# Row maxima on one core: six late rows moved from VectorE to TensorE and GpSimd, and the loads cut to 22

## The chip, the cores and the metric

The kernel runs on one core of a Trainium2 chip. The metric is the device time of one execution in microseconds (us); lower is better. Beside it stands the span: the time from the first to the last instruction that the profile of that execution shows. The time is longer than the span; the difference is called "outside the span". Faster or slower needs 2%.

## The reference

```python
# x: float32 [32, 512, 1024]
def reference(x):
    return np.max(x, axis=-1).astype(np.float32)      # [32, 512]
```

There are 16,384 rows of 1,024 values, 67.1 MB. They lie over 128 partitions, 128 rows on each. Below, "a row" means one row on each partition: 512 KB and one column of the result.

## The kernel before

All of x passes once through a ring of 45 rows in SBUF. Each load brings n rows, and VectorE reduces a whole load in one instruction. The loads get smaller so that little is left to do when the last one lands; the last row comes in two halves.

```python
BLOCKS = [
    [14, 13, 12, 11, 9, 8, 8, 7, 6, 5, 5, 4, 4, 3, 3],
    [2, 2, 2, 1, 1, 1, 1, 1, 1, 1, 1, 1],
]
RING = 45
# ...
        for n in loads:
            if at + n > RING:
                at = 0
            xc = ring[:, at:at + n, :]
            nc.sync.dma_start(out=xc, in_=xb[:, b:b + n, :])
            reduce = nc.vector.reduce_max(out=res[:, first + b:first + b + n], in_=xc, axis=X)
            at += n
            b += n
# ... the last row in two halves, then two small stores of the result
```

Of the kernel before, what the change touches and what calls it, by code (L numbers as in the profile page):

```python
# [1 line left out]

# [4 lines left out]


F32 = mybir.dt.float32



BLOCKS = [
    [14, 13, 12, 11, 9, 8, 8, 7, 6, 5, 5, 4, 4, 3, 3],
    [2, 2, 2, 1, 1, 1, 1, 1, 1, 1, 1, 1],
]
RING = 45
SYNC = mybir.DependencyInfo(mybir.DependencyClass.Sync, mybir.DependencyReason.DATA)


@with_exitstack
def kernel(
    ctx: ExitStack,
    tc: tile.TileContext,
    x: bass.AP,
    out: bass.AP,
):
    nc = tc.nc
    P = 128
    X = mybir.AxisListType.X  # L30

    xf = x.flatten_outer_dims()
    N, D = xf.shape
    H = D // 2
    I = N // P
    of = out.flatten_outer_dims()

    once = ctx.enter_context(tc.tile_pool(name="once", bufs=1))
    ring = once.tile([P, RING, D], F32)
    res = once.tile([P, I], F32)  # L40

    PAD = 16
    tail = once.tile([P, PAD + H], F32)

    at = first = 0
    views = []
    for loads in BLOCKS:
        S = sum(loads) + (loads is BLOCKS[-1])
        xb = xf[first * P:(first + S) * P, :].rearrange("(p i) d -> p i d", p=P)
        dst = bass.AP(tensor=of.tensor, offset=of.offset + first * P, ap=[[S, P], [1, S]])  # L50
        views.append((dst, res[:, first:first + S]))
        b = 0
        for n in loads:
            if at + n > RING:
                at = 0
            xc = ring[:, at:at + n, :]
            nc.sync.dma_start(out=xc, in_=xb[:, b:b + n, :])  # L57
            reduce = nc.vector.reduce_max(out=res[:, first + b:first + b + n], in_=xc, axis=X)  # L58
            at += n
            b += n  # L60
        first += S
    assert first == I

    if at + 1 > RING:
        at = 0
    half = ring[:, at, :H]
    nc.sync.dma_start(out=half, in_=xb[:, b, :H])
    nc.sync.dma_start(out=tail[:, PAD:], in_=xb[:, b, H:])
    nc.vector.reduce_max(out=tail[:, PAD - 1:PAD], in_=half, axis=X)  # L69
    nc.vector.reduce_max(out=res[:, I - 1:], in_=tail[:, PAD - 1:], axis=X)  # L70


    store = nc.scalar.dma_start(out=views[0][0], in_=views[0][1])
    tc.add_manual_dep(store.ins, reduce.ins.name, SYNC, reason="behind the loads")
    nc.scalar.dma_start(out=views[1][0], in_=views[1][1])


# [1 line left out]
_INS = ['x']  # L79
_OUTS = [((32, 512), 'float32')]  # L80


# [23 lines left out]
```

## Time and profile before

| | before |
|---|---|
| time, median | 165.02 us (6 runs, 164.87 to 165.15) |
| span | 163.4 us |
| VectorE busy | 139.0 us in 29 instructions |
| input stream, first to last byte | 1.72 to 159.29 us |
| last reduction ends | 161.07 us |

How to read it: neither share of busy time decides. VectorE (DVE in the profile) is busy for 85% of the span, but nearly all its idle time (20.3 of 22.1 us) lies at the start, before the first load has landed. The input stream occupies the 16 DMA engines almost from start to end (96.6% of the span, queue q1 of the page). What counts is which of the two finishes last: VectorE, at 161.07 us, less than 2 us behind the last byte. After it come the store of the result and the end of the program, 2.3 us. The lines are shown in the prediction.

### The profile page before, as it was taken

To read this page: it belongs to the slowest core of one execution; us is meant where nothing else is said; L and a number is where in the kernel's file an instruction comes from. 1 tells how busy PE (TensorE), PEld (TensorE's weight loads), DVE (VectorE), ACT (ScalarE), POOL (GpSimd) and SP (SyncE) were. 2 spreads that over 40 slices of the span, in tenths; PEclk is the share of its full clock that TensorE was granted. 3 is DMA by queue.
4 is the path that set the end of the run, shared out by engine and by line. 5 is a ranking of instruction groups with operands and counts; after the bars stand their busy time and mean duration, and the time that the engine had idled before them with its cause. 6 is when DMAs were issued, how large, how long until landed. Compare 5 with 4: busy or idle time off the path is not lost.

```text
span 163.4 us, 117 instructions
## 1 busy us (share of the span) xinstructions
DVE 139.0 (85%) x29; POOL 0.2 (0%) x4
## 2 busy tenths in 40 slices
DVE  0000099989998999999999999999999999999994
POOL 0000000000000000000000000000000000000000
DMA  6999999999989989999989999999999999999990
GB/s 225 449 449 449 433 417 417 417 401 529 433 385 430 452 386 432 433 433 441 457 385 481 401 442 422 409 438 421 446 409 425 437 410 422 427 407 409 409 355 16
DMA packets 4464, 67.18 MB, mean 411 GB/s; under 512 B 752, under 2 KB 752, under 8 KB 2160
## 3 DMA queue, kind: packets, MB, share of 16 engines
q1 hardware_dynamic: 4176, 67.11, 96.6%
q10 hardware_dynamic: 288, 0.07, 0.2%
HBM read 67.11 MB, written 0.07 MB: 411 GB/s over the span
## 4 chain that ended last, share of the span: by engine, by line
DVE 49%; DMA 48%; SPq 1%; issue 0%
DMA ring<-in_x_dram 48%; DVE res L58 48%; SPq L57 1%; DVE res L70 0%; DVE tail L69 0%
## 5 line engine op out<-in xcount | busy, mean ns | idle before, releaser
L58 DVE TENSOR_REDUCE res<-ring 128x1 f32<-128x1024 f32 (+12 forms) x27 | 137.7, 5165 | 22.1 <-DMA ring<-in_x_dram 22.1
L70 DVE TENSOR_REDUCE res<-tail 128x1 f32<-128x513 f32 x1 | 0.7, 686 | 0.0
L69 DVE TENSOR_REDUCE tail<-ring 128x1 f32<-128x512 f32 x1 | 0.7, 682 | 0.0
L90 POOL MEMSET const-bfloat16-1.0<- 128x1 bf16 x1 | 0.1, 102 | 0.0
L90 POOL MEMSET const-uint8-127<- 128x1 uint8 x1 | 0.1, 102 | 0.0
L90 POOL MEMSET const-float32-0.0<- 128x1 f32 x1 | 0.1, 99 | 0.2 <-issue 0.2
L90 POOL MEMSET const-float32-1.0<- 128x1 f32 x1 | 0.1, 99 | 0.0
## 6 DMA issues: line engine op xcount, KB each, us to landing
ring<-in_x_dram SPq DMA_DIRECT2D x2, 4096.0 KB, 25.6
ring<-in_x_dram SPq DMA_DIRECT2D x1, 7168.0 KB, 19.6
ring<-in_x_dram SPq DMA_DIRECT2D x1, 6656.0 KB, 34.9
ring<-in_x_dram SPq DMA_DIRECT2D x1, 6144.0 KB, 48.9
ring<-in_x_dram SPq DMA_DIRECT2D x1, 5632.0 KB, 28.5
ring<-in_x_dram SPq DMA_DIRECT2D x2, 2560.0 KB, 38.4
ring<-in_x_dram SPq DMA_DIRECT2D x1, 4608.0 KB, 24.7
ring<-in_x_dram SPq DMA_DIRECT2D x9, 512.0 KB, 13.8
```

Of the source, the lines that this page charges most:

```text
L57: nc.sync.dma_start(out=xc, in_=xb[:, b:b + n, :])
L58: reduce = nc.vector.reduce_max(out=res[:, first + b:first + b + n], in_=xc, axis=X)
L69: nc.vector.reduce_max(out=tail[:, PAD - 1:PAD], in_=half, axis=X)
L70: nc.vector.reduce_max(out=res[:, I - 1:], in_=tail[:, PAD - 1:], axis=X)
L90: nc = _bacc.Bacc("TRN2", target_bir_lowering=False, num_devices=1)
```

## The change

The intent is to take work from VectorE late in the kernel, where it is behind, by the three engines that stand idle (the page of the kernel before has no busy time on TensorE and ScalarE and 0.2 us on GpSimd). Each of six rows is turned on TensorE (eight transposes of 128x128, so that the values of one row lie across partitions), copied from PSUM to SBUF by ScalarE, reduced over partitions by GpSimd, and its 8 x 128 partial maxima are turned back on TensorE (eight one-column transposes). VectorE then reduces 8 values instead of 1,024. With less work, VectorE was to stand fewer and larger loads, 22 in place of 29.

```diff
 BLOCKS = [
-    [14, 13, 12, 11, 9, 8, 8, 7, 6, 5, 5, 4, 4, 3, 3],
-    [2, 2, 2, 1, 1, 1, 1, 1, 1, 1, 1, 1],
+    [(15, 0, -1), (15, 0, -1), (15, 0, -1), (15, 0, -1), (12, 0, -1), (7, 0, -1), (11, 0, -1), (10, 2, 8), (7, 0, -1), (5, 2, 13)],
+    [(4, 1, 15), (2, 0, -1), (2, 1, 18), (1, 0, -1), (1, 0, -1), (1, 0, -1), (1, 0, -1), (1, 0, -1), (1, 0, -1), (1, 0, -1)],
 ]
-RING = 45
+RING = 46
 ...
+    def by_gpsimd(rows, cols, m):
+        back = psmall.tile([P, m, C], F32)
+        for k in range(m):
+            ps = psum.tile([P, D], F32)
+            for c in range(C):
+                in_turn("PE", nc.tensor.transpose(out=ps[:, c * P:(c + 1) * P], in_=rows[:, k, c * P:(c + 1) * P], identity=ident))
+            sb = turn.tile([P, D], F32)
+            nc.scalar.copy(out=sb, in_=ps)
+            top = allr.tile([P, D], F32)
+            nc.gpsimd.partition_all_reduce(top, sb, P, bass_isa.ReduceOp.max)
+            run(backs)                 # turns back of the row before
+            backs.append(turn_back)    # turn_back: eight transposes of top[0:1, ...] into back[:, k, c]
+        return lambda: in_turn("DVE", nc.vector.reduce_max(out=cols, in_=back, axis=X))
 ...
             if m:
                 due.setdefault(w, []).append(by_gpsimd(...))
+            else:
+                run(backs)
+            if j == 0:
+                nc.gpsimd.tensor_copy(out=ident[:, 0:1], in_=xc[:, 0, 0:1])
+                make_identity(nc, ident)
```

A triple (n, m, w) means: load n rows, send the last m of them through the detour, and let VectorE take in their results after its reduction of load w. `in_turn` fixes the order of the instructions on TensorE and on VectorE.

More of the change, by code (lines that the diff above doesn't have):

```diff
@@ L6 @@
 from concourse._compat import with_exitstack
+from concourse import bass_isa
+from concourse.masks import make_identity
 F32 = mybir.dt.float32
 BLOCKS = [
-    [14, 13, 12, 11, 9, 8, 8, 7, 6, 5, 5, 4, 4, 3, 3],
-    [2, 2, 2, 1, 1, 1, 1, 1, 1, 1, 1, 1],
-]
-RING = 45
+    [(15, 0, -1), (15, 0, -1), (15, 0, -1), (15, 0, -1), (12, 0, -1), (7, 0, -1), (11, 0, -1), (10, 2, 8), (7, 0, -1), (5, 2, 13)],
+    [(4, 1, 15), (2, 0, -1), (2, 1, 18), (1, 0, -1), (1, 0, -1), (1, 0, -1), (1, 0, -1), (1, 0, -1), (1, 0, -1), (1, 0, -1)],
+]
+RING = 46
+NOSYNC = mybir.DependencyInfo(mybir.DependencyClass.NoSync, mybir.DependencyReason.DATA)
 SYNC = mybir.DependencyInfo(mybir.DependencyClass.Sync, mybir.DependencyReason.DATA)
@@ L34 @@
     H = D // 2
+    C = D // P
     I = N // P
@@ L38, with in_turn, turn_back, run @@
     once = ctx.enter_context(tc.tile_pool(name="once", bufs=1))
+    turn = ctx.enter_context(tc.tile_pool(name="turn", bufs=2))
+    allr = ctx.enter_context(tc.tile_pool(name="allr", bufs=2))
+    psum = ctx.enter_context(tc.tile_pool(name="psum", bufs=3, space=bass.MemoryType.PSUM))
+    psmall = ctx.enter_context(tc.tile_pool(name="psmall", bufs=2, space=bass.MemoryType.PSUM))
     ring = once.tile([P, RING, D], F32)
     res = once.tile([P, I], F32)
+    ident = once.tile([P, P], F32)
     PAD = 16
     tail = once.tile([P, PAD + H], F32)
-    at = first = 0
+    backs = []
+    due = {}
+    before = {}
+    def in_turn(engine, inst):
+        if engine in before:
+            tc.add_manual_dep(inst.ins, before[engine].ins.name, NOSYNC, reason="in turn")
+        before[engine] = inst
+        return inst
+    def by_gpsimd(rows, cols, m):
[3 more added lines that the diff above has]
+            for c in range(C):
+                in_turn("PE", nc.tensor.transpose(
+                    out=ps[:, c * P:(c + 1) * P],
+                    in_=rows[:, k, c * P:(c + 1) * P],
+                    identity=ident,
+                ))
+            sb = turn.tile([P, D], F32)
[3 more added lines that the diff above has]
+            run(backs)
+            def turn_back(top=top, k=k):
+                for c in range(C):
+                    in_turn("PE", nc.tensor.transpose(
+                        out=back[:, k, c:c + 1],
+                        in_=top[0:1, c * P:(c + 1) * P],
+                        identity=ident[0:1, 0:1],
+                    ))
+            backs.append(turn_back)
+        return lambda: in_turn("DVE", nc.vector.reduce_max(out=cols, in_=back, axis=X))
+    def run(calls):
+        while calls:
+            calls.pop(0)()
+    at = first = j = 0
     views = []
     for loads in BLOCKS:
-        S = sum(loads) + (loads is BLOCKS[-1])
+        S = sum(n for n, m, w in loads) + (loads is BLOCKS[-1])
         xb = xf[first * P:(first + S) * P, :].rearrange("(p i) d -> p i d", p=P)
@@ L52 @@
         b = 0
-        for n in loads:
+        for n, m, w in loads:
             if at + n > RING:
@@ L57 @@
             nc.sync.dma_start(out=xc, in_=xb[:, b:b + n, :])
-            reduce = nc.vector.reduce_max(out=res[:, first + b:first + b + n], in_=xc, axis=X)
+            cols = res[:, first + b:first + b + n]
+            if m:
+                due.setdefault(w, []).append(by_gpsimd(xc[:, n - m:, :], cols[:, n - m:], m))
+            else:
[3 more added lines that the diff above has]
+                make_identity(nc, ident)
+            if n > m:
+                reduce = in_turn("DVE", nc.vector.reduce_max(
+                    out=cols[:, :n - m], in_=xc[:, :n - m, :], axis=X))
+            run(due.get(j, []))
             at += n
             b += n
+            j += 1
         first += S
     assert first == I
-    if at + 1 > RING:
-        at = 0
     half = ring[:, at, :H]
@@ L68 @@
     nc.sync.dma_start(out=tail[:, PAD:], in_=xb[:, b, H:])
-    nc.vector.reduce_max(out=tail[:, PAD - 1:PAD], in_=half, axis=X)
-    nc.vector.reduce_max(out=res[:, I - 1:], in_=tail[:, PAD - 1:], axis=X)
+    in_turn("DVE", nc.vector.reduce_max(out=tail[:, PAD - 1:PAD], in_=half, axis=X))
+    in_turn("DVE", nc.vector.reduce_max(out=res[:, I - 1:], in_=tail[:, PAD - 1:], axis=X))
     store = nc.scalar.dma_start(out=views[0][0], in_=views[0][1])
```

## The prediction

> **What bounds the kernel now.** I read the busy shares by slice first, then the chain that ended last in order of time, then the groups of instructions kept apart by shape, then the busy time by stage, and last the single DMA packets.
>
> The page's slices (columns: forty equal slices of 4.1 us, busy share in tenths):
>
> ```profile
> DVE  0000099989998999999999999999999999999994
> DMA  6999999999989989999989999999999999999990
> ...
> q1 hardware_dynamic: 4176, 67.11, 96.6%
> ```
>
> Two rows are full at once. The DMA engines run from the first slice to the last, VectorE from the sixth. Neither has a hole that the other could be moved into. The chain that ended last, in order of time (start, length, what):
>
> ```profile
> 1.63 48.93 DMA ring<-in_x_dram
> 50.56 0.02 issue
> 50.58 12.96 DVE res L58
> ...
> 63.94 30.30 DMA ring<-in_x_dram
> 94.24 0.02 issue
> 94.27 65.48 DVE res L58 x21
> 159.75 0.60 DVE tail L69
> 160.35 0.02 issue
> 160.38 0.69 DVE res L70
> ```
>
> Up to 94.24 us the path goes through the DMA, after it through VectorE alone. So VectorE sets the end: 21 reductions back to back without a wait, done at 161.07 us. But the DMA is close behind. The single packets show the last data byte of the input at 159.29 us, after 1.72 us for the first, and the 16 engines idle for under 0.8 us in between. The last half row was issued at 150.77 us and took 9.0 us to land, so it landed at 159.77 us. Had VectorE been infinitely ahead, its last half-row reduction of 0.69 us would have ended near 160.5 us. **Taking work from VectorE can win about 0.6 us** before the stream takes over. In the groups below (columns: busy us, mean ns, idle time before and what ended it) most of its idle time, 20.3 of 22.1 us, is the wait for the first load.
>
> ```profile
> L58 DVE TENSOR_REDUCE res<-ring 128x14 f32<-128x14336 f32 x1 | 15.1, 15086 | 20.3 <-DMA ring<-in_x_dram 20.3
> L58 DVE TENSOR_REDUCE res<-ring 128x1 f32<-128x1024 f32 x9 | 10.2, 1215 | 0.0
> L70 DVE TENSOR_REDUCE res<-tail 128x1 f32<-128x513 f32 x1 | 0.7, 686 | 0.0
> ```
>
> Rates from here: (15,086 - 1,215)/13 = 1.067 us a row, plus about 0.15 us an instruction, of which some 0.09 overlap with the next when nothing is waited for (1-row reductions start every 1.125 us).
>
> ```profile
> 100.00:150.00 50.00, 50.00 (x13) 0.00 (x0) 1.00 1.00 421
> ```
>
> In this stage (columns: stretch, length, DVE busy, POOL busy, PE clock, DMA share, GB/s) both are at 100%.
>
> [...]a 57,344-byte packet takes 2.115 us, 27.1 GB/s an engine, 434 for 16. A 4,096-byte packet takes 0.161 us (407 GB/s), so a packet costs some 0.010 us beside its bytes.
> [...]
> [...]
> [...]
>
> **The change, part by part.**
> *DMA stream.* The bytes stay. 29 loads become 22, at 8 packets per engine each: 56 packets fewer per engine, by 0.010 us: **-0.5 us**. A row per partition is 8 packets of 4,096 bytes, 1.204 us; a load adds 0.08. The first load took 1.3 us longer than that (18.2 us for 14 rows); I keep that. The new stream ends at about 158.8 us and the last half row lands at about 159.2 (0.4 to 0.5 us after its last byte). I walked the ring of 46 rows through: the fourth load waits for the first reduction, at 37.7 us, but the second and third keep the queue full until 57.4; no later load is short either, nor does the limit of 8 loads in flight that the issues wait for bite. The stream stays unbroken.
>
> *VectorE's start.* The first load has 15 rows, not 14: it lands at 21.6, 1.2 us later. The first four loads are all of 15. The DMA needs 18.1 us for each, VectorE 16.15, so VectorE waits 2.0 us before each of the second, third and fourth (landings 39.7, 57.8, 76.0). In the kernel before, shrinking loads left it only 0.65, 0.51, 0.38 and 0.21. VectorE is then idle for 21.6 + 5.9 + some 0.4 later = 27.9 us against 22.1: **+5.8 us**.
>
> *VectorE's work.* Six rows leave: 6 x 1.067 = 6.4 us. The 27 big reductions become 20. Their fixed part is 2.2 us before (139.0 less 127 rows at 1.067 and the two halves, 1.3 net), and 4 x 0.15 + 16 x 0.06 = 1.6 after: -0.6. Four little reductions of the turned-back maxima come in, 16 or 8 values each, estimated at 0.16 us: +0.65. Together **-6.4 us** (139.0 to 132.6).
>
> *Sum.* From 92.1 us (end of the fourth reduction) VectorE has 62 rows left: 66.1, plus 18 instructions at 0.06, plus 0.65, plus 0.4 of waits: end at 160.4, against 161.07. The two sums agree: -6.4 + 5.8. So **-0.65 us if the six maxima arrive in time**. Time: 164.99 - 0.65 = 164.3 us.
>
> *The detour.* Each late row costs 8 turns on TensorE (p), a ScalarE copy of 1,024 columns (c[...]), the all-reduce (T) and 8 one-column turns back (b). VectorE's order is fixed, so it stands still if a result is late. The order of instructions shows the tight place. The two rows of the 5-row load land at 139.0; GpSimd then does rows 3, 4 and 5 in a row; the turns of row 6 stand on TensorE behind row 5's turn back; so row 6 is done at 139.0 + 4T + 2(p + c + b)[...]. VectorE reaches that place at 157.8.[...] The other three places leave more: the first two rows (landing 124.4, wanted at 140.6)[...]. Beyond the limit each further microsecond of T costs 4 us, straight on the end.
>
> **Rivals.**
> *1. GpSimd becomes the bound.* For: VectorE's order is fixed, the last detour is serial[...]; with T = 3.5 the end moves 2 to 3 us (166 to 167.5 us), with 5 some 8 us (172)[...]. Against: whoever put the waits where they are left two rows 15 us and the last one 9, which only makes sense with an all-reduce of 2 to 3.5 us known[...].
> *2. The DMA stream bounds anyway.* Then the end can't come before 159.2 + 0.7 = 159.9 us, and the time not below about 163.8. This caps the gain at 1.2 us, 0.7%, whatever GpSimd does. It is the strongest statement here, since it rests on packets alone.
> *3. The new waits early eat all of it.* If VectorE's idle time grows by more than 6 us (say because landings of 15-row loads are noticed later), the end goes back to 161 and the time to 165. It nearly does this already.
> *4. The DMA gets slower beside PE, ScalarE and GpSimd traffic*[...]: 1% would be 1.6 us. Nothing before speaks for it.
>
> **Range and chances.** Rivals 2 and 3 put the time between 163.8 and 165.0 if the results are in time, to which I give some two thirds. A late last row by up to 3 us, still within 2%, gets one in seven; more than that one in six. A gain over 2% (below 161.7) would need the stream itself to shrink by 2 us, which the packets exclude except by a different start. My value is 164.4 us, range 163.6 to 168.0; faster 0.02, same 0.81, slower 0.17.
>
> **What would show it.** Right: VectorE's busy time near 132.6 us and its idle time near 28, with three waits of about 2 us before 76 us; last input byte near 158.8 us; no wait of VectorE on TensorE; VectorE's last instruction ending near 160.4. Wrong: a wait of VectorE for TensorE in front of the small reductions, the last above all (then T, p or b is above the estimate, and the GpSimd rows show by how much); a DMA row with slices below 9 (a starved queue, my walk through the ring is wrong); longer 1,024-column reductions beside GpSimd (contention after all). The prediction fails as a whole if the all-reduce takes over 4 us.

The 0.16 us for a small reduction follows from the 0.15 us an instruction and the 1.067 us a row (0.15 to 0.17 us in the changed kernel). The limit in "The detour" came to T of at most 2.9 us, and the sizes put in for p, c, b and the steps from engine to engine are estimates with no trace behind them. "The limit" and "T = 3.5" refer to these 2.9 us. The limit of 8 loads in flight is in the traces: counted from issue to last landing, 8 are the most at any time in the kernel before and in the changed one.

## The result

| | before | changed |
|---|---|---|
| time, median of 6 | 165.02 us | 169.38 us (168.21 to 170.24) |
| ratio of the fast runs | 1 | 1.0252, interval 1.0211 to 1.0294: slower |
| span, profiled run | 163.4 us | 166.9 us |
| outside the span | 1.8 us | 1.9 to 2.9 us |
| VectorE busy | 139.0 us | 132.6 us |
| last byte of the input | 159.29 us | 159.34 us |
| last reduction ends | 161.07 us | 164.58 us |

A ratio here is the mean time of one kernel's fast runs over that of the other's of the same rounds, so not quite the ratio of the medians quoted beside it. The result is correct. The predicted range, 163.6 to 168.0 us, does not hold the time.

The slices of the page of the changed kernel (forty of 4.2 us, busy share in tenths) and its input queue:

```profile
PE   0000000000000000000000000000008125382520
...
DVE  0000089993999599986999999999999999999914
...
POOL 0000000000000000000000000000002930777250
...
DMA  6999879999979999989989999989999899999900
...
q1 hardware_dynamic: 3168, 67.11, 94.3%
```

VectorE's row shows three dips that were not there (the waits for the 15-row loads, 2.6, 2.1 and 2.0 us) and a hole of nearly a whole slice just before the end. In that place the DMA row is already at 0: nobody waits for data there.

The groups by shape (busy us, mean ns of one, idle time before and what ended it):

```profile
L124 DVE TENSOR_REDUCE res<-ring 128x15 f32<-128x15360 f32 x4 | 64.6, 16153 | 28.1 <-DMA ring<-in_x_dram 28.1
L83 POOL PARTITION_ALL_REDUCE top<-sb x6 | 19.3, 3254 | 108.9 <-ACT sb L81 108.9
L81 ACT COPY sb<-ps 128x1024 f32<-128x1024 f32 x6 | 6.1, 1012 | 149.5 <-PE ps L75 149.5
L95 DVE TENSOR_REDUCE res<-back 128x1 f32<-128x8 f32 x2 | 0.3, 160 | 3.5 <-PE back L88 3.5
```

One all-reduce takes 3.25 us. The last line is the hole: VectorE stood still for 3.5 us in front of one reduction of 8 values, waiting for TensorE's turns back. The timeline of that stretch, from the fifth row's result on (start, length, engine, line; in brackets the idle time before):

```profile
153.55 1.01 PE L88 MATMUL back<-ident,top 1*128 1x1 f32 x8 [3.17 <-POOL top L83]
154.49 1.97 PE L75 MATMUL ps<-ident,ring 128*128 128x128 f32 x8
...
156.55 1.01 ACT L81 COPY sb<-ps 128x1024 f32<-128x1024 f32 x1 [6.37 <-PE ps L75]
157.65 3.22 POOL L83 PARTITION_ALL_REDUCE top<-sb  x1 [4.16 <-ACT sb L81]
160.93 1.01 PE L88 MATMUL back<-ident,top 1*128 1x1 f32 x8 [4.47 <-POOL top L83]
161.97 0.17 DVE L95 TENSOR_REDUCE res<-back 128x1 f32<-128x8 f32 x1 [3.49 <-PE back L88]
```

The data of the sixth row had landed by 150.06 us, when VectorE took the load's other row without a wait. Its turns start only at 154.49, behind the fifth row's turns back, because TensorE's order says so; GpSimd idles for 4.16 us meanwhile; and from there one step follows the other with nothing beside it. The chain that ended last goes through exactly these pieces, where in the kernel before it was VectorE alone:

```profile
160.93 1.02 PE back L88 x8
161.95 0.02 issue
161.97 0.04 DVE res L95
162.01 0.04 issue
162.06 1.21 DVE res L124
163.27 0.60 DVE tail L136
163.87 0.02 issue
163.89 0.69 DVE res L137
```

Two things remain beside the hole. Without the 3.5 us the last reduction would have ended at 164.58 - 3.49 = 161.09 us, no earlier than before, while the prediction had 160.4. And between the profiled runs the time grew by 4.3 us (165.17 to 169.49) but the span by 3.5: the other 0.8 us (0.1 to 1.2 over the six runs, 0.6 on average) lie outside it. The experiments take up the hole and these two.

### The profile page after: what moved, and what is told of

It reads as the page before. It is cut to its first block, busy times and chain, and to the rows that moved or that the text cites. A ratio compares the mean times of both kernels' runs of the same rounds, so it can differ in the third digit from the quotient of the medians.

```text
span 166.9 us, 329 instructions
## 1 busy us (share of the span) xinstructions
PE 16.6 (10%) x96; PEld 14.8 (9%) x96; DVE 132.6 (79%) x26; ACT 7.4 (4%) x7; POOL 20.2 (12%) x13
## 4 chain that ended last, share of the span: by engine, by line
DMA 56%; DVE 29%; POOL 4%; PE 4%; issue 3%; POOLq 2%; ACT 1%; SPq 0%; ACTq 0%
DMA ring<-in_x_dram 56%; DVE res L124 28%; POOL top L83 4%; PE ps L75 2%; POOLq L168 2%; ACT sb L81 1%; PE back L88 1%; DVE res L137 0%; DVE tail L136 0%; SPq L113 0%; DVE res L95 0%; ACTq L81 0%
## 5 line engine op out<-in xcount | busy, mean ns | idle before, releaser
L124 DVE TENSOR_REDUCE res<-ring 128x1 f32<-128x1024 f32 (+7 forms) x20 | 131.3, 6599 | 28.4 <-DMA ring<-in_x_dram 28.3
L83 POOL PARTITION_ALL_REDUCE top<-sb x6 | 19.3, 3254 | 108.9 <-ACT sb L81 108.9
L75 PE MATMUL ps<-ident,ring 128*128 128x128 f32 x48 | 11.0, 418 | 129.1 <-DMA ring<-in_x_dram 129.1
L75 PEld LDWEIGHTS ps<-ident,ring 128*128 128x128 f32 x48 | 9.6, 224 | 129.1 <-issue 125.2
L81 ACT COPY sb<-ps 128x1024 f32<-128x1024 f32 x6 | 6.1, 1012 | 149.5 <-PE ps L75 149.5
L88 PE MATMUL back<-ident,top 1*128 1x1 f32 x48 | 5.7, 235 | 16.3 <-POOL top L83 16.3
L88 PEld LDWEIGHTS back<-ident,top 1*128 1x128 f32 x48 | 5.2, 201 | 17.9 <-POOL top L83 17.9
L95 DVE TENSOR_REDUCE res<-back 128x2 f32<-128x16 f32 (+1 forms) x4 | 0.6, 162 | 3.5 <-PE back L88 3.5
masks.py:199 POOL TENSOR_SCALAR_AFFINE_SELECT ident<-ident 128x128 f32<-128x128 f32 x1 | 0.3, 282 | 10.5 <-issue 10.5
```

Of the source, the lines that this page charges most:

```text
L75: in_turn("PE", nc.tensor.transpose(out=ps[:, c * P:(c + 1) * P], in_=rows[:, k, c * P:(c + 1) * P], identity=ident,))
L81: nc.scalar.copy(out=sb, in_=ps)
L83: nc.gpsimd.partition_all_reduce(top, sb, P, bass_isa.ReduceOp.max)
L88: in_turn("PE", nc.tensor.transpose(out=back[:, k, c:c + 1], in_=top[0:1, c * P:(c + 1) * P], identity=ident[0:1, 0:1],))
L95: return lambda: in_turn("DVE", nc.vector.reduce_max(out=cols, in_=back, axis=X))
L124: reduce = in_turn("DVE", nc.vector.reduce_max(out=cols[:, :n - m], in_=xc[:, :n - m, :], axis=X))
```

## The experiments

Theory: the loss has three parts, the sixth row's detour in series (on TensorE's order), an input stream that is slower beside GpSimd's preparation, and something of the new engines' programs that acts outside the span. GpSimd's preparation stands for what its records show in the changed kernel before the first row comes: MODIFY_POOL_CONFIG at 21.95 us, GpSimd standing still for 10.5 us, the identity, and MODIFY_POOL_CONFIG again at 32.90. Rivals: GpSimd as a whole is too slow whatever the order; the large loads are bad (or good) in themselves; traffic of TensorE and ScalarE slows the DMA.

All results below were correct. The table has one profiled run of each kernel; "row 45 by" is when 45 rows' worth of bytes had arrived by the single DMA packets, the bytes of a packet spread evenly over its time.

| kernel | row 45 by | last byte | last reduction ends | span | outside | time, median | ratio to before |
|---|---|---|---|---|---|---|---|
| before | 57.06 | 159.29 | 161.07 | 163.4 | 1.8 | 165.02 | 1 |
| changed | 57.33 | 159.34 | 164.58 | 166.9 | 2.6 | 169.38 | 1.0252 |
| e1_order | 57.34 | 159.69 | 161.44 | 163.7 | 2.6 | 166.25 | 1.0076 |
| e2_plan_only | 57.01 | 158.76 | 166.12 | 168.4 | 1.8 | 170.14 | 1.0312 |
| e3_old_plan | 57.28 | 160.27 | 162.24 | 164.6 | 2.2 | 166.13 | 1.0074 |
| e4_library | 56.98 | 159.19 | 160.95 | 163.3 | 1.8 | 165.02 | 1.0000 |
| e5_const_ident | 57.07 | 158.93 | 160.64 | 163.0 | 2.6 | 165.35 | 1.0027 |
| e6_pe96 | 57.04 | 160.50 | 162.33 | 164.7 | 1.8 | 166.39 | 1.0083 |
| e7_pe48 | 57.01 | 159.04 | 160.82 | 163.2 | 1.7 | 165.61 | 1.0042 |
| e8_switch | 57.33 | 160.42 | 162.27 | 164.6 | 1.8 | 165.93 | 1.0063 |
| e9_two_rows | 57.01 | 159.33 | 161.07 | 163.4 | 1.8 | 165.16 | 1.0015 |
| e10_one_row | 57.03 | 159.20 | 160.99 | 163.3 | 1.7 | 165.15 | 1.0012 |
| e11_plan24 | 56.98 | 158.99 | 160.67 | 163.2 | 1.8 | 165.06 | 1.0007 |

The medians of before in the other calls were 164.91 to 165.01 us.

### e1_order: the sixth row's turns ahead of the fifth row's turns back

```diff
-            else:
+            elif j != 11:
                 run(backs)
```

> Only the order on TensorE changes: the 8 turns of the last late row go ahead of the turn back of the row before it. Theory A (the span grew because the last row's detour stands in series behind the fifth row's, 3.5 us of VectorE standing still): the last all-reduce starts right after the fifth, near 153.5 instead of 157.65 us, its result is back near 157.8, VectorE reaches that place at 158.5 and does not wait; its last reduction ends near 161.1 (164.6 in the changed kernel), span 163.4 to 163.5, time 165.2 to 166.2. Rival B (GpSimd as a whole is the bound, whatever TensorE's order): the wait shrinks by less than half or moves to the fifth row's place, the end stays above 162.5.

The timeline of the same stretch:

```profile
150.63 6.43 POOL L83 PARTITION_ALL_REDUCE top<-sb  x2 [0.95 <-ACT sb L81]
...
157.11 1.01 PE L88 MATMUL back<-ident,top 1*128 1x1 f32 x8 [2.20 <-POOL top L83]
158.75 0.16 DVE L95 TENSOR_REDUCE res<-back 128x1 f32<-128x8 f32 x1
```

The sixth row's turns start at 150.67. The fifth and sixth all-reduce now follow each other without a gap, the result is there at 158.12, and VectorE takes it in at 158.75 without a wait. The last reduction ends at 161.44 us. Theory A holds and rival B falls: with the same GpSimd work, one changed place in TensorE's order brings the time from 169.38 to 166.25 us. End, span and time came out 0.1 to 0.3 us above what was expected. The span is only 0.3 us longer than the one before, yet the time is still 1.3 us longer.

### e2_plan_only: the new loads, all rows on VectorE

```diff
-    [(15, 0, -1), ..., (10, 2, 8), (7, 0, -1), (5, 2, 13)],
-    [(4, 1, 15), (2, 0, -1), (2, 1, 18), ...],
+    [(15, 0, -1), ..., (10, 0, -1), (7, 0, -1), (5, 0, -1)],
+    [(4, 0, -1), (2, 0, -1), (2, 0, -1), ...],
-            if j == 0:
-                nc.gpsimd.tensor_copy(out=ident[:, 0:1], in_=xc[:, 0, 0:1])
-                make_identity(nc, ident)
```

> The new plan of 22 loads alone, every row on VectorE, no TensorE, ScalarE or GpSimd work. Theory A (the plan costs VectorE about 6 us of early waits, which the six rows only pay back): waits of 2 to 2.8 us before the second, third and fourth reduction as in the changed kernel, then 68 rows from 92.7 us: the last reduction ends at 166 to 167, span 168.5 to 169.5, time 170.3 to 171.3. Rival (fewer, larger loads are themselves a gain): time at or below 165. Second question: by row 45 the input stream of the changed kernel was 0.27 us behind that of the kernel before[...]; if the large packets did it, it stays.

VectorE's waits for data, from the list of waits (us in total, times, longest), in the kernel before and here:

```profile
DVE res L58 <- DMA ring<-in_x_dram: 22.1, 5, 20.3
...
DVE res L120 <- DMA ring<-in_x_dram: 27.7, 5, 21.6
```

The last reduction ends at 166.12 us, 5.05 later than before: the plan of large equal loads costs VectorE 5.6 us of waits (27.7 against 22.1) and six rows' relief is spent on that. Theory A holds; span and time came out 0.1 to 0.2 us below its ranges. The plan's gain is real but small: the last byte comes at 158.76, 0.53 us earlier than before, as 56 packets fewer per engine should give at 0.010 us each. These are single traces: those of the old loads without slow packets (before, e4_library, e7_pe48) have the last byte at 159.04 to 159.29, so the gain is 0.3 to 0.5 us. And the second question has an answer: without the detour the stream is not behind at row 45 (57.01), so the packets' size is not what delayed it in the changed kernel.

### e3_old_plan: the old loads, six rows through the detour

```diff
-    [(15, 0, -1), (15, 0, -1), ...
+    [(14, 0, -1), (13, 0, -1), (12, 0, -1), (11, 0, -1), (9, 1, 7), (8, 1, 8), (8, 1, 9), (7, 1, 10), (6, 1, 11), (5, 1, 12), ...
```

> The kernel before's shrinking loads, with one row of each of the loads 5 to 10 through the detour, early enough that nobody waits for it. Theory A (the input stream ends at 159.3 and its last landing near 159.8 whatever VectorE does): VectorE now waits for data, its last reduction ends near 160.5 (161.07 before), span 162.8, so at most 0.6 us less; with the time outside the span as in the changed kernel (0.8 us more than before) the time is 164.4 to 165.4, a tie. Rival (VectorE's work was what set the end): 6 us less work gives 3 us or more, time below 162.

Half a miss. With 6 us of work fewer VectorE gained nothing, so the rival falls; but the end came later than theory A said, 162.24 instead of 160.5 us, and the time was 166.13 instead of 164.4 to 165.4. The table shows one reason: the stream itself was late, by 0.22 us at row 45 and by a full microsecond at the last byte. A load has landed only when the slowest of the 16 engines has delivered its share (the trace has 16 landings for each load; those of the first load of the kernel before come from 19.67 to 20.29 us, and its reduction starts at 20.31): 120 rows' worth of bytes were in only 0.2 us late. The chain shows the other:

```profile
85.44 37.86 DMA ring<-in_x_dram
123.31 0.02 issue
123.33 5.49 DVE res L124
```

From this landing on VectorE works to the end without a wait; in the kernel before, the same reduction starts at 122.29 us. All six rows came from loads that land earlier, so the time that they freed went into waits (28.9 us in place of 22.1). That the stream's end set the end, as theory A had it, is therefore not shown by this run; e9_two_rows takes the point up.

### e4_library: one unused all-reduce at the start of the kernel before

```diff
+    nc.gpsimd.memset(idle, 0.0)
+    nc.gpsimd.partition_all_reduce(spare, idle, P, bass_isa.ReduceOp.max)
```

> The kernel before with one all-reduce of a zeroed 128x128 tile at the start, its result unused. It asks where the 0.8 us come from that the changed kernel's time has outside its span (169.49 - 166.9 = 2.6 against 165.17 - 163.4 = 1.8).[...] If TensorE's or ScalarE's part does it: time 165.0, as before.[...]

Two conditions gave 165.6 to 166.0 us if GpSimd's part makes the 0.8 us, and a row-45 mark 0.2 to 0.3 us later if it slows the stream.

Nothing moved: time 165.02, outside 1.8, stream as before. The all-reduce started at 1.06 us, about 0.1 us after MODIFY_POOL_CONFIG (0.9 to 1.0 us), with no pause between:

```profile
1.06 0.70 POOL L50 PARTITION_ALL_REDUCE spare<-idle  x1
```

So an all-reduce by itself brought no pause here. The changed kernel has one: its trace has a MODIFY_POOL_CONFIG ahead of the instruction that builds the identity (21.9 to 22.0 us), another ahead of the first all-reduce (32.9), and GpSimd paused for 10.5 us after the first of them. What it does in the pause no record shows.

### e8_switch: GpSimd's preparation alone, in the kernel before

```diff
+            if b == 0 and first == 0:
+                nc.gpsimd.tensor_copy(out=ident[:, 0:1], in_=xc[:, 0, 0:1])
+                make_identity(nc, ident)
+                nc.gpsimd.partition_all_reduce(spare, ident, P, bass_isa.ReduceOp.max)
```

> The kernel before with only GpSimd's part of the change at its old place: the identity is built after the first load, then one all-reduce of it, unused; no TensorE or ScalarE work. Theory A[...]: slow packets within 10 us of each change, the stream 0.2 to 0.3 us behind at row 45 and to the end, its last byte at 159.6 to 160.3, last reduction ending at 161.2 to 162.2 (161.07 before), span 163.6 to 164.6. Outside the span: 1.76 if TensorE's program makes that part[...]. Rival B: all as before.

(Outside the span 2 to 2.9 us if GpSimd's preparation makes that part.)

```profile
DVE res L64 <- DMA ring<-in_x_dram: 23.3, 5, 20.2
...
POOL spare L68 <- issue: 11.2, 1, 11.2
POOL ident masks.py:199 <- issue: 10.9, 1, 10.9
```

There are two pauses of GpSimd, 10.9 us before the identity is made and 11.2 before the all-reduce. In the DMA packets of just those stretches some are slow: at 25.2 us three of 53,248 bytes took 0.54 to 0.75 us longer than the usual 1.97, and at 37.4 to 37.8 us three of 49,152 bytes 0.68 to 1.06 longer than 1.82. No packet of before, e2, e4 or e5 is over 0.06 us late between 15 and 48 us. In the changed kernel's own trace the slow packets are there, from 25.1 to 27.7 us and from 36.8 to 36.9, up to 0.72 us longer than the usual 2.27; here as there they begin 3 to 6 us after a MODIFY_POOL_CONFIG. The last byte moves from 159.29 to 160.42 us, the last reduction from 161.07 to 162.27, and the time from 164.94 to 165.93. Outside the span it stays at 1.8. Theory A holds: the stream is slower with GpSimd's preparation than without. By what means is not shown: the trace has no packets of GpSimd's at these places, and the link is inferred from when the slow packets occur.

### e5_const_ident: e1_order with the identity from a constant

```diff
-            if j == 0:
-                nc.gpsimd.tensor_copy(out=ident[:, 0:1], in_=xc[:, 0, 0:1])
-                make_identity(nc, ident)
+            if j == 2:
+                nc.sync.dma_start(out=ident, in_=eye.ap())     # eye: constant in HBM, 64 KB
```

> The kernel e1_order with the identity taken from a constant by one 64 KB load behind the third big one, so that GpSimd builds nothing[...]. Theory A ([...]slow packets at 25 to 30 and 36 to 40 us, 0.27 us at row 45 and 0.3 to 0.6 more at the slowest engine): no slow packets there, the second to fourth reductions start at 39.7, 57.9 and 76.1 as in e2_plan_only, last input byte near 158.9 (159.7 in e1_order), last reduction ends at 160.4 to 160.7 (161.44 in e1_order), span 162.7 to 163.0. The time outside the span stays at 2.3 to 2.9 if TensorE's program makes it (time 165.0 to 165.8)[...]. Rival B (TensorE or ScalarE traffic slows the stream): as e1_order, 166.2.

(1.8 us outside and 164.5 to 164.8 us if GpSimd's preparation makes the time outside.)

The chain that ended last:

```profile
158.05 0.07 DVE res L97
158.12 1.21 DVE res L124
159.33 0.60 DVE tail L136
159.93 0.02 issue
159.95 0.69 DVE res L137
```

There are no slow packets and no pause; the second to fourth reductions start at 39.65, 57.87 and 76.17 us; the last byte comes at 158.93 and the last reduction ends at 160.64 us, 0.43 before the old kernel's. Rival B falls: TensorE and ScalarE work here as in e1_order, and the stream runs within 0.2 us as without them (row 45 by 57.07 us, last byte at 158.93, against 57.01 and 158.76 in e2_plan_only). This is the change as it was meant, span 162.8 to 163.0 us against 163.1 to 163.3. Still the time is 165.35 us, 0.3% more than before, since 2.4 to 2.6 us lie outside the span.

### e6_pe96 and e7_pe48: unused TensorE work in the kernel before

```diff
+    nc.gpsimd.memset(zero, 0.0)
+    for _ in range(96):            # 48 in e7_pe48
+        nc.tensor.matmul(out=turned, lhsT=zero, rhs=zero, start=True, stop=True)
```

> The kernel before with 96 unused matmuls of a zero tile at the start: as many TensorE instructions as the changed kernel. Theory A (the time outside the span grows because TensorE's longer program makes the engine fetch 16 KB of instructions after the end, as the packet 1.7 us behind the span of the changed kernel shows): that packet appears, time outside the span 2.0 to 2.9 (1.76 before), total 165.3 to 166.0, span 163.3 as before.[...]

> The same with 48 matmuls. Theory A: with half the instructions[...] no packet behind the end, outside 1.76, total 165.0. If the packet and the time stay, the number of instructions is not it[...].

The packet that theory A goes by is in the changed kernel's trace: 16,384 bytes of the kind "instruction", at 168.60 us, 1.7 us behind the span; that TensorE's program brings it was the theory. The rival of e6_pe96 is: the time outside comes from GpSimd (outside 1.76, total 165.0).

Both expectations missed in a telling way. The edit does not do quite what they say: each of their fp32 matmuls stands in the trace as two, so e6_pe96 has 192 TensorE matmuls, twice the changed kernel's 96, and e7_pe48 has 96, as many as it. The DMA records show, beside the data:

```
kernel          packet of 16,384 bytes, kind "instruction" (start, length in us)    span
changed         168.60  1.12                                                        166.9
e1_order        165.46  1.03                                                        163.7
e3_old_plan     166.08  0.93                                                        164.6
e5_const_ident  164.77  1.09                                                        163.0
e6_pe96          15.46  0.95                                                        164.7
e7_pe48         163.79  1.38                                                        163.2
before, e2, e4, e8, e9, e10, e11: none inside or after the span
```

In e6_pe96 it came in the middle of the first load: one packet of that load was 0.50 us late, the first load landed 1.3 us later,

```profile
DVE res L65 <- DMA ring<-in_x_dram: 23.4, 5, 21.6
```

and VectorE ran late by that much to the end (last reduction at 162.33 us). The time outside stayed at 1.8. In e7_pe48 the four runs disagree: spans of 163.2, 163.2, 164.7 and 163.5 us with 1.7, 2.7, 1.8 and 1.8 us outside. So each kernel with 96 or more TensorE matmuls in its trace has one such packet. In e6_pe96 it fell into the stream and cost time inside the span, in e7_pe48's profiled run behind the span and cost hardly any; that its moment also explains the other three runs of e7_pe48 is the author's guess, as they have no trace. That the packet goes with TensorE's work is shown by which kernels have it (e9_two_rows to e11_plan24 use ScalarE and GpSimd too, with at most a third of the TensorE work, and have none); that it is what fills the extra 0.8 us outside is a reading, not more: in e7_pe48's profiled run the packet is there behind the span, and the time outside is 1.7.

From how much TensorE work on the packet comes, and by what means, no run here shows: e9_two_rows, with 32 transposes, has none, and e7_pe48, with 96 matmuls in the trace, has one.

### e9_two_rows and e10_one_row: few rows, the old loads

```diff
(in short)
-BLOCKS: e3_old_plan's, six rows
+BLOCKS: (8, 1, 7) and (7, 1, 9) alone      # e10_one_row: (8, 1, 8) alone
 and the identity from a constant, as in e5_const_ident
```

> The best that the findings allow with little TensorE work: the kernel before's loads, one row of the sixth and one of the eighth load through the detour, identity from a constant. VectorE has 2 rows less, so the stream sets the end: last byte at 159.4 to 159.5 (64 KB more), last reduction ends at 160.5 to 160.8 (161.07 before), span 162.6 to 163.0. If the 64 TensorE instructions cause no fetch behind the end, the time is 164.4 to 164.8, some 0.2 to 0.3% less than before. If they do, outside 2.5 and the time 165.2 to 165.5: then no number of rows pays.

> The same with one row, of the seventh load: 32 TensorE instructions. VectorE's last reduction ends at 160.5 to 160.8 here too, since one row (1.07 us) is more than the 0.6 us that the stream leaves. Time 164.4 to 164.8 without a fetch behind the end, 165.2 to 165.5 with one. Rival: a tie with before, 164.9 to 165.1, the gain of the span given back outside.

The time outside is 1.7 to 1.9 us in all ten runs, as hoped. But the last reductions end at 161.07 and 160.99 us, as before, and the times, 165.16 and 165.15, miss the 164.4 to 164.8 hoped for. The chain of e9_two_rows says why:

```profile
85.54 36.76 DMA ring<-in_x_dram
122.30 0.02 issue
122.32 37.44 DVE res L124 x17
```

The rows were taken from loads that land at 85 and 103 us. VectorE used the free time to wait for the next loads and was back in its old place at 122.3 us (in the kernel before, the same reduction starts at 122.29); the rest of the run is unchanged. Only rows that land after about 122 us relieve the end here.

### e11_plan24: a last attempt

```diff
(in short)
+BLOCKS: 15, 15, 13, 12, 10, 9, 7, 7, 7, 5, 4, 5, 3, 3, 2, 2, then eight of 1;
+        one row each of the 12th and 14th load through the detour, identity from a constant
```

> A last attempt at a version that beats both: 24 loads and the two halves (15, 15, 13, 12, 10, 9, 7, 7, 7, 5, 4, 5, 3, 3, 2, 2, then eight of 1), identity from a constant, and two truly late rows, of the 12th and 14th load, through the detour (64 TensorE instructions, no fetch behind the end in e9_two_rows). By the rates of the traces the stream ends at 159.1, 0.2 us earlier than before, and VectorE's last reduction at 160.6 to 160.9 (161.07 before): span 162.8 to 163.1, time 164.6 to 164.8, 0.1 to 0.2% less than before. Rival: a tie, as e9_two_rows, since the ends of stream and of VectorE are within what one plan or another can move.

The last reduction ends at 160.67 us, 0.4 earlier, but the span's end moves by less (163.2 to 163.5 us over the runs) and the time is 165.06 against 165.01: a tie, as its rival said, interval 0.9993 to 1.0021. No version found beats the kernel before.

## Why the prediction was wrong

By its own steps:

- **VectorE's work: right.** 132.6 us predicted, 132.6 measured. No reduction got longer beside GpSimd: the 1-row ones took 1,211 ns (1,215 before).
- **VectorE's start: right in mechanism.** Three waits of 2.0 us predicted; 2.6, 2.1 and 2.0 in the changed kernel. In e2_plan_only and e5_const_ident, without GpSimd's preparation, the starts are those predicted to within 0.2 us.
- **DMA stream: half right.** Fewer packets saved 0.3 to 0.5 us of the 0.5 (e2_plan_only). In the changed kernel most of it was lost again beside GpSimd's preparation. That this could slow the data loads was in rival 4, dismissed with "Nothing before speaks for it". e8_switch puts it at 1.0 us of time alone, e5_const_ident against e1_order at 0.9.
- **The detour: the step that failed, on sizes.** The formula was right, and so was the place named in it. It asked for T of at most 2.9 us, with estimates for p, c and b. Measured: T = 3.25, p = 1.97, c = 1.01, b = 1.01. T alone adds 4 x 0.35 = 1.4 us; 2(p + c + b) is 7.98, another 1.8 above the estimates. With the landing at 139.7 (not 139.0) and 0.5 us in all from engine to engine (0.04 to 0.09 a step in the timeline) the formula gives 139.7 + 13.0 + 8.0 + 0.5 = 161.2; measured 161.94, as GpSimd did not do rows 3, 4 and 5 quite in a row: it also stood 0.95 us before the fifth, whose turns were behind the third row's turns back in the same way. VectorE was there at 158.48 (157.8 predicted), so it stood still for 3.5 us where no wait was predicted. These 3.5 us, the 0.7 us by which VectorE came later and the 0.8 us more outside the span make up the 5.0 us between the predicted 164.4 and the measured time. No run before the prediction had shown an all-reduce; it took 3.25 us for 128x1024, and 0.70 for 128x128 in e4_library. e1_order proves the mechanism by removing it. The argument that whoever placed the waits must have known T was the reason for giving this rival only one chance in three; the placement was simply too tight by 3.5 us, or by one place in TensorE's order.
- **Rival 1's size for T = 3.5** (2 to 3 us at the end) was too small for the same reason: it rested on the same estimates.
- **Missing from the sum:** more time outside the span. None was predicted; it came to 0.1 to 1.2 us.
- **The cap by the stream: holds.** No kernel measured ends its last reduction before 160.64 us or takes under 164.8.
- **"Taking work from VectorE can win about 0.6 us"** lacked a condition: it must be work on rows that land late (e9_two_rows).

The parts, as ratios to before: order on TensorE 1.0252 - 1.0076, about 2.9 us of 165; GpSimd's preparation 1.0076 - 1.0027, 0.8; the remaining 1.0027 is 0.8 us outside less 0.3 us of span gained. They add up to the 4.2 us of the ratio 1.0252 by construction; each is what its edit brought with the others in place.

## What to carry to other kernels

When work moves to idle engines, write down the whole detour of the last item against the moment at which it is needed, with the fixed order of every engine on the way: a turn back queued ahead of a turn cost more here than all else. Look where the transfers end before counting what a relieved engine saves; here the most there was to win was under 1% and each of the helpers' side costs (GpSimd's preparation, 0.8 us; the instruction packet that comes with TensorE's work, 1.3 us in e6_pe96) was as large. And relief counted here only after the last point where the engine waits for data (122.3 us in e9_two_rows).
